# Rewriting the gated mixer of a two-layer decoder trunk: modulation in quarters, v with tokens on partitions, an fp32 spatial product

## The chip, the cores and the metric

The kernel runs on one core of a Trainium2 chip. The metric is the device time of one execution in microseconds; the median of several runs counts. Before the change the median of three runs is 2674.6 us (2672.22, 2674.6 and 2674.74).

## What is computed

A trunk of two layers on one sequence of 1024 tokens, 1024 channels wide, all in float32. Layer 0 mixes tokens with a gated MLP (gMLP), layer 1 with attention; each mixer is followed by a squared-ReLU MLP. Every sub-layer is modulated by shift, scale and gate rows that come from a conditioning vector `c`. The change is in the mixer of layer 0 alone:

```python
def ada_mod(c, w, b):
    m = jax.nn.silu(c) @ w + b                 # w: 1024 x 3072
    shift, scale, gate = jnp.split(m, 3, axis=-1)
    return shift[:, None, :], scale[:, None, :], 1.0 + gate[:, None, :]

def mixer_a(h, w_in, b_in, vn_g, vn_b, w_s, b_s, w_out):    # h = x * (1 + scale) + shift
    uv = jax.nn.gelu(h @ w_in + b_in)          # w_in: 1024 x 2048
    u, v = jnp.split(uv, 2, axis=-1)
    v = layer_norm(v, vn_g, vn_b)              # over the 1024 channels of a token
    v = v.reshape(B, S // CHUNK, CHUNK, A_GROUPS, A_GROUP_DIM)   # 8 chunks of 128 tokens, 16 groups of 64
    w_causal = jnp.where(causal, w_s, 0.0)     # 16 x 128 x 128, lower triangles
    z = jnp.einsum('gts,bnsgc->bntgc', w_causal, v) + b_s.T[:, :, None]
    return (u * z.reshape(B, S, A_WIDTH)) @ w_out

# the sub-layer: x = layer_norm(ALPHA * x + gate * mixer_a(h, ...))
```

## The kernel before, in words

Products of full precision are made of three fp32r matmuls: each operand is split into a high part (a cast, `split`, L100 to L103, the cast on ACT and the difference on DVE by default) and a low part, and hi·hi, hi·lo and lo·hi are summed in PSUM (`passes`, L345). The attention further on also uses plain fp32 matmuls (L1451, L1473, L1518, L1558); L1558 has 64 columns of stationary operand and writes alternately to the lower and the upper 64 partitions of a bank. Transposes are fp32 matmuls against an identity.

The mixer (L506 to L703) goes through these stages:

- **Modulation** (`ada_steps`, L110 to L183, and `mods`, L547). Shift and scale of sub-layer 0 are made in two halves of 512 channels. For each part and half, eight blocks of 128x512 of `ada_w` are loaded by SP and added on DVE, weighted by a column of silu(c) (L125, L128); the sum over partitions is then made on PE with 16 two-column matmuls of the split sum against ones (L162, L163).
- **h transposed.** `build_hT` (L210) transposes `x` on PE, applies scale and shift on ACT while it leaves PSUM (L221) and splits it. This is done for half 0 of the tokens (512 of them), four channel blocks after each half of the modulation, and then for half 1.
- **v.** `v_unit` loads and splits 128 columns of `w_in`; `v_sum` (L522) multiplies with the weights stationary, so v comes out with channels on partitions; `v_end` (L531) applies bias and GELU on ACT, transposes v back on PE (L536), copies it to `vz` on DVE (L537) and takes the statistics (L541). Units 0 to 3 go first for half 0, then half 1; units 4 to 7 follow for both halves.
- **Normalization and spatial product.** `norm_v` (L627) normalizes `vz` in two channel halves with gain and bias rows, mostly on DVE. `spatial(g)` (L639) splits one group of `vz`, multiplies it by the transposed triangle (three fp32r matmuls into `psz`, 512 columns each), and ACT writes it back to `vz` with the bias.
- **u and gating.** `u_unit` (L649) makes 128 channels of u, channels on partitions. `gate_unit` (L660) transposes z on PE (L667) and multiplies by u on DVE (L668).
- **Output product.** `OutRows` (L456) multiplies u·z by `w_out`; its matmuls are named `psd_wout`. After it comes the MLP.

In the background run further modulation steps (`later`, `tick`, L190 to L197): 88 steps, 64 of which load a block of 256 KB into a ring of two buffers and add it on DVE. `tick(6)` stands after each of the v units 4 to 7 and `tick(7)` in each `u_unit`.

The order of instructions on each engine is fixed when the program is built: a list scheduler places them by its own estimates of their times, except those marked with `tc.keep_in_program_order`, which stay in the order in which they are written. On the chip every engine and SP's queue of transfers go through their lists in that order and wait where an operand isn't ready. PSUM holds three banks called `tr` (transposes and small sums) and five called `mm` (products).

## Time and profile before

| | before |
|---|---|
| median of 3 runs | 2674.6 us (2672.22 to 2674.74) |
| profiled execution, its own time | 2670.79 us |
| its span in the profile | 2669.1 us, mean granted clock 0.991 |
| first v product starts | 26.03 us |
| first `psd_wout` matmul starts | 269.68 us |

The page of the profile gives, per engine, busy time and number of instructions. A timeline row reads: start and length in us, engine, line, operation, output tile and inputs, shapes, count; in brackets the idle time of the engine ahead of it and what ended that. A matmul's row lasts longer than the engine is taken by it, because matmuls are pipelined: its price in a dense stretch is the distance between starts. A row of a table by windows gives the stretch and its length, busy time and number of instructions of PE, PEld (weight loads), DVE, ACT and POOL, and at the end the granted clock of PE, the share of the transfer engines and the GB/s moved.

### The profile page before, as it was taken

The page shows a single profiled execution, that of the slowest core. Times are in us where ns is not written, and L with a number is a line of the kernel's source. Part 1 is how long each engine was busy: PE and PEld are TensorE (multiplying, and loading weights), DVE is VectorE, ACT ScalarE, POOL GpSimd, SP SyncE. Part 2 cuts the span into 40 slices and gives each one's busy share as a digit, 9 for nine tenths or more (in the row PEclk, how much of TensorE's full clock was granted, in tenths as well). Part 3 has the DMA queues.
Part 4 walks back from the last instruction along what each step waited for, and adds up shares of the span by engine and source line. Part 5 has one row for each costly group of instructions (what it writes and reads, how often), then busy time and mean ns, then how long its engine had stood idle before and what let it go on. Part 6 is the DMA issues. An engine that isn't in the chain of part 4 may idle for free. (4 is left out here: it accounts for less than half of the span.)

```text
span 2669.1 us, 36556 instructions
## 1 busy us (share of the span) xinstructions
PE 2587.4 (97%) x13114; PEld 2073.9 (78%) x13114; DVE 1933.7 (72%) x3490; ACT 1269.0 (48%) x2456; POOL 208.5 (8%) x225
## 2 busy tenths in 40 slices
PE   6999999999999998999999999999999999999998
PEld 5777878888788887887777777777776888878887
DVE  6786798787788777443676777767658865677887
ACT  3334376555443445322555555556426555543432
POOL 1011100000000000111122221111100000000000
PEclk9999999999999999999999999999999999999999
DMA  8533326666875643543344454444862654494562
GB/s 269 156 114 117 119 104 233 216 213 222 293 249 174 219 145 125 174 158 103 104 136 121 124 156 121 140 138 130 279 213 102 218 194 147 158 332 163 178 204 87
DMA packets 329771, 457.04 MB, mean 171 GB/s; under 512 B 51388, under 2 KB 176740, under 8 KB 329588
## 3 DMA queue, kind: packets, MB, share of 16 engines
q1 hardware_dynamic: 316532, 408.55, 47.7%
q0 software_dynamic: 13056, 46.14, 4.8%
q8 instruction: 103, 1.69, 0.3%
q14 instruction: 80, 0.66, 0.1%
HBM read 346.00 MB, written 108.61 MB: 170 GB/s over the span
## 5 line engine op out<-in xcount | busy, mean ns | idle before, releaser
L1365 PE MATMUL psqk<-right,left 128*128 128x512 f32 x2016 | 524.3, 405 | 3.3 <-DVE left L103 2.2
L1365 PEld LDWEIGHTS psqk<-right,left 128*128 128x128 f32 x2016 | 364.1, 189 | 97.0 <-issue 15.6
L857 PE MATMUL psua<-right,left 128*128 128x512 f32 x1536 | 364.2, 390 | 3.2 <-ACT right L102 1.7
L1015 PE MATMUL psd<-rhi,lhi 128*128 128x512 f32 x896 | 351.7, 392 | 2.1 <-ACT part L888 2.1
L1015 PE MATMUL psd<-rlo,lhi 128*128 128x512 f32 x896 | 351.0, 392 | 0.3 <-DVE rlo L103 0.2
L1015 PE MATMUL psd<-rhi,llo 128*128 128x512 f32 x896 | 350.9, 392 | 0.0
L857 PEld LDWEIGHTS psua<-right,left 128*128 128x128 f32 x1536 | 287.0, 188 | 65.1 <-ACT right L102 2.6
L103 DVE TENSOR_TENSOR left<-ws,left 128x512 fp32r<-128x512 f32 x224 | 163.2, 730 | 145.8 <-ACT left L102 143.9
L1432 ACT ACTIVATE p<-p,stat 128x256 f32<-128x256 f32 (+2 forms) x384 | 161.8, 423 | 154.5 <-DVE stat L1430 153.7
L1209 PE MATMUL psv<-vwhi,right 128*128 128x512 f32 x672 | 210.6, 395 | 7.2 <-ACT right L102 7.2
L1015 PEld LDWEIGHTS psd<-rhi,lhi 128*128 128x128 f32 x896 | 169.4, 189 | 38.1 <-ACT part L888 3.0
L1015 PEld LDWEIGHTS psd<-rlo,lhi 128*128 128x128 f32 x896 | 169.4, 189 | 36.0 <-DVE rlo L103 1.0
L1015 PEld LDWEIGHTS psd<-rhi,llo 128*128 128x128 f32 x896 | 169.6, 189 | 35.4
L857 PE MATMUL psuc<-right,left 128*128 128x512 f32 x768 | 188.2, 391 | 0.5 <-ACT right L102 0.4
L102 ACT CAST left<-ws 128x512 fp32r<-128x512 f32 x224 | 138.5, 619 | 97.8 <-DVE ws L778 78.7
L128 DVE SCALAR_TENSOR_TENSOR adaacc<-adaw,silu_c,adaacc 128x512 f32<-128x512 f32 x168 | 132.5, 798 | 65.5 <-DMA adaw<-in_ada_w_dram 65.0
L857 PEld LDWEIGHTS psuc<-right,left 128*128 128x128 f32 x768 | 143.4, 188 | 30.9 <-DVE right L103 0.9
L1209 PEld LDWEIGHTS psv<-vwhi,right 128*128 128x128 f32 x672 | 126.4, 189 | 35.6 <-ACT right L102 7.6
L103 DVE TENSOR_TENSOR llo<-lraw,lhi 128x1024 fp32r<-128x1024 f32 x112 | 136.3, 1217 | 1.3 <-ACT lhi L102 1.3
L1209 PE MATMUL psv<-vwlo,right 128*128 128x512 f32 x336 | 132.1, 394 | 0.2 <-DVE vwlo L103 0.2
L1430 DVE CUSTOM_DVE_ANT_0 p<-sc,bias 128x256 f32<-128x256 f32 (+2 forms) x384 | 103.3, 324 | 39.9 <-PE sc L1518 39.9
L102 ACT CAST lhi<-lraw 128x1024 fp32r<-128x1024 f32 x112 | 117.3, 1048 | 7.0 <-PE psua L857 4.3
(267 smaller groups left out, 4452.9 us busy)
## 6 DMA issues: line engine op xcount, KB each, us to landing
lraw<-forms SPq DMA_DIRECT2D x112, 512.0 KB, 4.0
adaw<-in_ada_w_dram SPq DMA_DIRECT2D x192, 256.0 KB, 3.0
up<-in_mlp_w_up_dram SPq DMA_DIRECT2D x64, 512.0 KB, 3.7
forms<-s SPq DMA_DIRECT2D x128, 256.0 KB, 2.5
rraw<-in_mlp_w_down_dram SPq DMA_DIRECT2D x64, 512.0 KB, 4.3
forms<-part SPq DMA_DIRECT2D x96, 256.0 KB, 2.4
vraw<-in_b_w_qkv_dram SPq DMA_DIRECT2D x42, 512.0 KB, 3.8
spill<-acc SPq DMA_DIRECT2D x24, 512.0 KB, 2.7
```

What stands on the lines that cost most here:

```text
L102: first = A.copy(hi, src) if hi_engine is A else hi_engine.tensor_copy(hi, src)
L103: return first, lo_engine.tensor_tensor(lo, src, hi, op=ALU.subtract)
L128: ins = V.scalar_tensor_tensor(acc[:], raw[:], silu_c[:, k : k + 1], acc[:], ALU.mult, ALU.add)
L857: T.matmul(acc, w[:, a, k, :], right[p][:, b, k, :], start=p in (1, 2, 5) and k + a + b == 0, stop=k == 3 and a == 1, skip_group_check=True)
L1015: T.matmul(sums[kind, m][:], l[a][:, k, m * P : (m + 1) * P], r[b][:, k, :], start=p in (1, 5, 2, 3) and kp + k + a + b == 0, stop=kp == K ...
L1209: T.matmul(sums[own, m][:], right[p][:, b, 2 * kp + k, m * P : (m + 1) * P], w[a][:, k, :], start=new and k + a + b == 0, stop=kp + k == 2 ...
L1365: ins = T.matmul(sums[kind][:], w[:, a, k, :], right[p][:, b, k, :], start=p in (1, 2, 5) and k + a + b == 0, stop=k == 3 and a == 1, skip ...
L1430: V.tensor_tensor_reduce(out=pr, in0=src, in1=bias, scale=-0.125, scalar=3e38, op0=ALU.add, op1=ALU.min, accum_out=nm)
L1432: A.activation(pr, pr, AF.Exp, bias=nm, scale=-1.0, accum_out=l)
```

## The change

Shift and scale are made in four quarters of 256 channels. A block is now two rows of 128x256. Of the eight k rows of a quarter DVE adds five; the other three go to PE as fp32 matmuls with the raw 128x128 block stationary and one column of silu(c) moving, summed in PSUM with the DVE part against a column of ones: 16 matmuls for a quarter. All of the first stage (loads, sums, transposes, scaling, splits, the first products) is pinned in its written order.

v is made with tokens on partitions: hT is now the stationary operand and the weights move (`v_sums`), so that no transposing back is needed; the bias is added by DVE from PSUM and GELU runs in place. v is normalized without gain and bias; the gain becomes a column factor and the bias a row sum of the triangle (`shifts`) where z is used. The spatial product is one fp32 matmul per group and chunk with v (64 columns) stationary and the triangle moving, which gives z with channels on partitions; the two groups of a unit go to the two halves of the partitions.

The core of the diff (`ada_steps` loses its special case for sub-layer 0, `build_hT` is gone, `ones_f` is a tile of ones):

```diff
+            def v_split(dh, kk, raw, pin=free):
+                w_units[dh, kk] = [wts.tile([P, 2, HALF], F32R, name=f"winv_{dh}_{kk}_{m}", tag=f"w{m}") for m in ("hi", "lo")]
+                for ins in split(*(t[:] for t in w_units[dh, kk]), raw[:]):
+                    pin(ins)
+            def v_sums(half, dh, k, pin=free):
+                w = w_units[dh, k // 2]
+                for i in range(4):
+                    if k == 0:
+                        sums[half, dh, i] = bank("mm", f"psv_{dh}_{4 * half + i}")
+                    for a, b in ((0, 0), (0, 1), (1, 0)):
+                        pin(T.matmul(sums[half, dh, i][:], hT[half][a][:, k, i * P : (i + 1) * P], w[b][:, k % 2, :],
+                                     start=k == 0 and a + b == 0, stop=k == KD - 1 and a == 1))
+            def v_end(half, dh, stats=True):
+                w = slice(dh * HALF, (dh + 1) * HALF)
+                for i in range(4):
+                    z = vz[:, 4 * half + i, w]
+                    V.tensor_tensor(z, sums.pop((half, dh, i))[:], v_bias[:, w], op=ALU.add)
+                    A.activation(z, z, AF.Gelu_apprx_tanh)
+                    V.bn_stats(st_v[:, 4 * half + i, dh, :], z)
...
+                def load(q):
+                    def block(kk, part):
+                        t = raws[q, part, kk] = ada0.tile([P, 2, QUARTER], F32, name=f"adaw_0_{q}_{part}_{kk}", tag="adaw", bufs=16)
+                        c0 = part * D + q * QUARTER
+                        pin(nc.sync.dma_start(t[:], ada_w[0, 0, kk * QUARTER : (kk + 1) * QUARTER, c0 : c0 + QUARTER]
+                                              .rearrange("(k p) n -> p k n", p=P)))
+                    for kk in range(3):
+                        for part in (1, 0):
+                            block(kk, part)
+                    w = slice(q * QUARTER, (q + 1) * QUARTER)
+                    for i in range(4):
+                        pin(nc.sync.dma_start(tiles[i][:, w], x_in[i * P : (i + 1) * P, w]))
+                    w_raw[q] = v_raw(0, q)
+                    for part in (1, 0):
+                        block(3, part)
...
+                def total(q):
+                    pst = bank("tr", f"psa_0_{q}")
+                    for part in range(2):
+                        for n in range(2):
+                            c = slice(2 * part + n, 2 * part + n + 1)
+                            w = slice(n * P, (n + 1) * P)
+                            for k in range(ON_DVE, KD):
+                                pin(T.matmul(pst[:, c], raws[q, part, k // 2][:, k % 2, w], silu_c[:, k : k + 1], start=k == ON_DVE, stop=False))
+                            pin(T.matmul(pst[:, c], accs[q, part][:, w], ones_f[:, 0:1], start=False, stop=True))
...
+                load(0)
+                add(0, range(ON_DVE))
+                load(1)
+                for q in range(4):
+                    total(q)
+                    psts = [turn(0, k, tiles, pin) for k in (2 * q, 2 * q + 1)]
+                    h = scaled(0, 2 * q, psts[0], pin)
+                    high(0, 2 * q, h, pin)
+                    if q:
+                        v_sums(0, 0, 2 * q - 1, pin)
+                    if q < 3:
+                        add(q + 1, range(2))
+                    low(0, 2 * q, h, pin)
+                    v_split(0, q, w_raw[q], pin)
+                    h = scaled(0, 2 * q + 1, psts[1], pin)
+                    high(0, 2 * q + 1, h, pin)
+                    if q < 3:
+                        add(q + 1, range(2, 3))
+                    low(0, 2 * q + 1, h, pin)
+                    v_sums(0, 0, 2 * q, pin)
+                    if q < 2:
+                        load(q + 2)
+                    if q < 3:
+                        add(q + 1, range(3, ON_DVE))
+                v_sums(0, 0, KD - 1, pin)
...
+                v_end(0, 0)
+                for k in range(KD):
+                    h = scaled(1, k, turn(1, k, others))
+                    high(1, k, h)
+                    low(1, k, h)
+                    v_sums(1, 0, k)
+                v_end(1, 0)
...
+                def shifts():
+                    for b in range(2):
+                        pst = bank("tr", f"psrow_{b}")
+                        for n in range(4):
+                            pair(lambda e, rows_: T.matmul(pst[rows_, n * P : (n + 1) * P], ones_f[:, 0:HEAD], wsT[:, 2 * (4 * b + n) + e, :],
+                                                           start=True, stop=True))
...
+                for half in (1, 0):
+                    for k in range(KD):
+                        if half and k % 2 == 0:
+                            v_split(1, k // 2, v_raw(1, k // 2))
+                        v_sums(half, 1, k)
+                        tick(2)
+                    if half:
+                        shifts()
+                    v_end(half, 1)
+                    norm_v(half)
...
                 def gate_unit(u, ut):
                     w = slice(u * P, (u + 1) * P)
+                    banks = []
+                    for half in (1, 0):
+                        p = bank("mm", f"psz_{u}_{half}")
+                        banks.append((half, p))
                         for n in range(4):
-                            T.transpose(pst[:, n * P : (n + 1) * P], vz[:, 4 * half + n, w], ident[:])
-                        V.tensor_tensor(vz[:, tiles, w], pst[:].rearrange("p (n c) -> p n c", c=P),
+                            pair(lambda e, rows_: T.matmul(p[rows_, n * P : (n + 1) * P], vz[:, 4 * half + n, (2 * u + e) * HEAD : (2 * u + e + 1) * HEAD],
+                                                           wsT[:, 2 * u + e, :], start=True, stop=True))
+                    for half, p in banks:
+                        t = work.tile([P, HALF], F32, name=f"zt_{u}_{half}", tag="h")
+                        t3 = t[:].rearrange("p (n c) -> p n c", c=P)
+                        V.scalar_tensor_tensor(t3, p[:].rearrange("p (n c) -> p n c", c=P), cols[:, o_s + u : o_s + u + 1],
+                                               shift[:, u, :].unsqueeze(1).to_broadcast([P, 4, P]), ALU.mult, ALU.add)
+                        V.tensor_tensor(vz[:, 4 * half : 4 * half + 4, w], t3,
                                         ut[:, half * HALF : (half + 1) * HALF].rearrange("p (n c) -> p n c", c=P), op=ALU.mult)
...
                 uts = [u_unit(0)]
                 for u in range(KD):
-                    for g in range(2 * u, 2 * u + (2 if u < 5 else 6)):
-                        if u <= 5:
-                            spatial(g)
-                    if u + 2 < KD:
-                        uts.append(u_unit(u + 2))
+                    if u + 1 < KD:
+                        uts.append(u_unit(u + 1))
                     gate_unit(u, uts[u])
```

`add(q, ks)` is the DVE sum over the k rows given (two parts, 128x256 each); `turn`, `scaled`, `high` and `low` are one channel block's transposes (PE), scaling (ACT), cast (ACT) and difference (DVE); `v_raw` loads 256x512 of `w_in` by SP; `norm_v(half)` normalizes four 128x1024 tiles on ACT. The output product and all that follows are unchanged.

More of the change, by code (lines that the diff above doesn't have):

```diff
@@ L208, in act_pair @@
         return tuple(act.tile([P, KD, HALF], F32R, name=f"{name}_{m}", tag="act") for m in range(2))
-    def build_hT(j, half, tiles, pair, ks=range(KD), pinned=False):
-        hi, lo = pair
-        for k in ks:
-            pst = bank("tr", f"pst_{j}_{half}_{k}")
-            for n, t in enumerate(tiles):
-                ins = T.transpose(pst[:, n * P : (n + 1) * P], t[:, k * P : (k + 1) * P], ident[:])
-                if pinned and n == 0:
-                    tc.keep_in_program_order(ins)
-            h = work.tile([P, HALF], F32, name=f"h_{j}_{half}_{k}", tag="h")
-            mul, add = ada[j]["mul", k // 4], ada[j]["add", k // 4]
-            A.activation(h[:], pst[:], AF.Identity, bias=add[:, k % 4 : k % 4 + 1], scale=mul[:, k % 4 : k % 4 + 1])
-            split(hi[:, k, :], lo[:, k, :], h[:], hi_engine=V if k % 2 else A)
-            yield
     def rstd_of(dst, var, n, name):
@@ L507, in mixer_a @@
         nonlocal ada_p, vec
+        QUARTER = 2 * P
         with ExitStack() as ph:
@@ L531, in v_end @@
-            def v_end(u, half):
-                vt = work.tile([P, HALF], F32, name=f"vt_{u}_{half}", tag="h")
-                A.activation(vt[:], sums[u, half][:], AF.Gelu_apprx_tanh, bias=cols[:, o_i + KD + u : o_i + KD + u + 1])
-                pst = bank("tr", f"psvt_{u}_{half}")
-                for n in range(4):
-                    T.transpose(pst[:, n * P : (n + 1) * P], vt[:, n * P : (n + 1) * P], ident[:])
-                V.tensor_copy(vz[:, 4 * half : 4 * half + 4, u * P : (u + 1) * P],
-                              pst[:].rearrange("p (n c) -> p n c", c=P))
-                if u % 2:
-                    for i in range(4 * half, 4 * half + 4):
-                        V.bn_stats(st_v[:, i, u // 2, :], vz[:, i, (u - 1) * P : (u + 1) * P])
@@ new lines, in v_end, with turn @@
+            def v_end(half, dh, stats=True):
[5 more added lines that the diff above has]
+                    V.bn_stats(st_v[:, 4 * half + i, dh, :], z)
+            def turn(half, k, tiles, pin=free):
+                pst = bank("tr", f"pst_0_{half}_{k}")
+                for n, t in enumerate(tiles):
+                    pin(T.transpose(pst[:, n * P : (n + 1) * P], t[:, k * P : (k + 1) * P], ident[:]))
+                return pst
@@ new lines, in scaled, with high, low @@
+            def scaled(half, k, pst, pin=free):
+                h = work.tile([P, HALF], F32, name=f"h_0_{half}_{k}", tag="h")
+                m = mods[k // 2]
+                pin(A.activation(h[:], pst[:], AF.Identity, bias=m[:, k % 2 : k % 2 + 1], scale=m[:, 2 + k % 2 : 3 + k % 2]))
+                return h
+            def high(half, k, h, pin=free):
+                pin(A.copy(hT[half][0][:, k, :], h[:]))
+            def low(half, k, h, pin=free):
+                pin(V.tensor_tensor(hT[half][1][:, k, :], h[:], hT[half][0][:, k, :], op=ALU.subtract))
@@ new lines, in shifts @@
+                def shifts():
[4 more added lines that the diff above has]
+                                                           start=True, stop=True))
+                        for n in range(4):
+                            u = 4 * b + n
+                            V.scalar_tensor_tensor(shift[:, u, :], pst[:, n * P : (n + 1) * P], cols[:, o_s + KD + u : o_s + KD + u + 1],
+                                                   shift[:, u, :], ALU.mult, ALU.add)
@@ L639, in spatial @@
-                def spatial(g):
-                    w = slice(g * HEAD, (g + 1) * HEAD)
-                    hi = a1.tile([P, NT, HEAD], F32R, name=f"vhi_{g}", tag="vhi", bufs=2)
-                    lo = a1.tile([P, NT, HEAD], F32R, name=f"vlo_{g}", tag="vlo", bufs=2)
-                    split(hi[:], lo[:], vz[:, :, w])
-                    p = bank("mm", f"psz_{g}")
-                    p3 = p[:].rearrange("p (n c) -> p n c", c=HEAD)
-                    passes(p3, [([t[:, g, :] for t in wsT], [hi[:], lo[:]])])
-                    A.activation(vz[:, :, w], p3, AF.Identity, bias=cols[:, o_s + g : o_s + g + 1])
+                    rstd_of(mv[:, 2, tiles], mv[:, 1, tiles], 4, f"r_v{half}")
```

203 lines of the change are left out of this document (84 added, 119 removed).

## The prediction

> **What bounds the kernel now.** The page comes first, for which engine is full; then a table by windows of the mixer's two parts (up to the last product of units 0 to 3 for half 0 of the tokens, and from there to the output product), of a stretch at half clock and of the output product.
>
> ```profile
> span 2669.1 us, 36556 instructions
> PE 2587.4 (97%) x13114; PEld 2073.9 (78%) x13114; DVE 1933.7 (72%) x3490; ACT 1269.0 (48%) x2456; POOL 208.5 (8%) x225
> ```
> ```profile
> 0.00:10.00 10.00, 0.45 (x1) 0.18 (x1) 3.92 (x11) 1.49 (x2) 0.70 (x6) 1.00 0.69 208
> 10.00:20.00 10.00, 0.73 (x3) 0.64 (x4) 8.63 (x13) 1.24 (x2) 0.00 (x0) 1.00 1.07 385
> 61.37:269.68 208.31, 195.03 (x937) 158.54 (x937) 158.00 (x251) 79.70 (x120) 28.63 (x17) 0.98 0.41 124
> 0.00:61.37 61.37, 38.58 (x163) 31.48 (x163) 39.83 (x61) 18.12 (x25) 10.92 (x10) 0.97 0.88 292
> 46.04:49.45 3.41, 3.41 (x18) 3.41 (x19) 0.70 (x3) 1.83 (x3) 0.00 (x0) 0.50 0.22 87
> 269.68:347.25 77.57, 77.57 (x343) 64.14 (x342) 57.59 (x102) 25.72 (x40) 7.78 (x3) 1.00 0.40 129
> ```
>
> PE is 97% busy, so time is saved only by taking work from PE or by filling its idle time. The output product has none of that: 342 matmuls of 512 columns in 77.57 us, **0.227 us** each, at full clock. The mixer ahead of it is different: in the first 61.37 us PE is busy for 38.58, since it waits for the modulation, whose loads keep the transfer engines 88% busy; in the next 208.31 it is busy for 195.03. Whatever moves the start of the output product (269.68 us) moves the end, since PE is dense behind it and nothing there waits for a clock of its own.
>
> **Part 1, the first stage.** Prices from the PE, ACT and DVE timelines: two-column sums, cold and warm; cold products; cold transposes; scaling, casts of 512 and of 1024 elements, the weight's low part, a 512-wide sum.
>
> ```profile
> 22.05 0.35 PE L162 MATMUL psa<-ones_r,adahi 128*128 128x2 f32 x1
> 22.26 0.35 PE L163 MATMUL psa<-ones_r,adalo 128*128 128x2 f32 x1
> 44.99 0.25 PE L162 MATMUL psa<-ones_r,adahi 128*128 128x2 f32 x1
> 45.10 0.25 PE L163 MATMUL psa<-ones_r,adalo 128*128 128x2 f32 x1
> 28.59 0.63 PE L528 MATMUL psv<-hT,winv_lo 128*128 128x512 f32 x1
> 29.02 0.63 PE L528 MATMUL psv<-hT,winv_hi 128*128 128x512 f32 x1
> 46.44 3.39 PE L216 MATMUL pst<-ident,x 128*128 128x128 f32 x16
> ```
> ```profile
> 23.84 1.63 ACT L221 ACTIVATE h<-pst,ada,ada 128x512 f32<-128x512 f32 x2 [0.56 <-PE pst L216]
> 25.37 0.61 ACT L102 CAST hT<-h 128x512 fp32r<-128x512 f32 x1
> 20.73 1.04 ACT L102 CAST winv_hi<-winv_raw 128x1024 fp32r<-128x1024 f32 x1 [1.14 <-DMA winv_raw<-in_a_w_in_dram]
> ```
> ```profile
> 6.74 0.74 DVE L128 SCALAR_TENSOR_TENSOR adaacc<-adaw,silu_c,adaacc 128x512 f32<-128x512 f32 x1
> 100.16 1.21 DVE L103 TENSOR_TENSOR winv_lo<-winv_raw,winv_hi 128x1024 fp32r<-128x1024 f32 x1
> ```
>
> Start to start, a two-column sum costs 0.21 us while the clock is at half and 0.11 at full clock, a product 0.43 against 0.227, a cold transpose 3.39/16 = 0.21.
>
> Data first. `total(0)` needs eight blocks of 256 KB, four slices of x of 128 KB and 512 KB of weights, 3.1 MB. The window rows moved 2.08 MB by 10 us and 385 GB/s after that, so the last block lands at about **13 us**. Later quarters need 3.1 MB per 8.2 us at that rate, and 16 buffers hold two quarters, so loads stay ahead. SP's queue is pinned with them: the loads of quarter 2 wait there for `total(0)` to free its buffers (near 20 us), and behind them stand the bias row, the column rows and x of half 1. These some 8.5 MB take 22 us at 385 GB/s, to 42 us, and the first that is needed, the bias row, is wanted at 63. Half as many elements in a row of the transfer could cost rate; the 512-byte rows of the old weight load lie in windows of the same GB/s, so I take none.
>
> Then PE. A `total` is 16 fp32 matmuls with a 128x128 stationary block each. The trace's only plain fp32 matmuls are in the attention, and there one source matmul leaves two records (below: 16 for 8). I price a total as 32 two-column sums: 32 x 0.21 = 6.7 us cold, 3.5 warm. From below it is 16 (half of that); I stay with 32 because the recorded weight loads double too.
>
> Quarter 0, cold: total ends at 13 + 6.7 = 19.7. Behind it lie, one after the other, the bias add with its handover (0.5), scaling 0.8, cast 0.6, weight cast 1.0 and the weight's low part 1.2 on DVE, behind which two half-width sums hide: 23.8. Twelve products at 0.43: **29**. Quarters 1 to 3, warm: 3.5 + 8 transposes (0.9 in all) + 24 products (5.5), and about 0.6 until the low part of the weights, which is pinned behind the cast of h, is there: 10.5 each, so 31.5. DVE needs per quarter ten half-width sums (0.4 each, from 0.74), two differences of 0.7 and one of 1.2, under 7 us, and stays under PE. The last twelve products: 2.7. Sum **63.2**, against 61.4 now.
>
> The clock can fall again. In the row 46.04:49.45 it is 0.50, after a wait and 32 two-column sums. The Trainium skill ("TensorE: Matmul & The Clock Gate", Part 1) says that about 3.4 us without enough activity halve the clock until a busy window has passed; this row's length of 3.41 us agrees, and the rule speaks against a stage that puts a 3.5 us train of one-column matmuls into each quarter. From the row: one such window costs up to 3.41/2 = 1.7 us. I put in 3 us for a late warm-up and one relapse: first stage **+5 us** (63.2 + 3 - 61.4), between -7 (totals at half price, which is 8.7 less, and no relapse) and +27 (the clock rival).
>
> **Part 2, from there to the output product.** What goes, in the PE timeline: transposes of z (those of v cost the same), spatial products, and four stalls.
>
> ```profile
> 203.61 1.03 PE L667 MATMUL pszt<-ident,vz 128*128 128x128 f32 x8
> 204.40 0.48 PE L350 MATMUL psz<-vhi,wsT 128*128 128x512 f32 x1
> 205.88 0.63 PE L350 MATMUL psu<-hT,winu_hi 128*128 128x512 f32 x2
> ```
> ```profile
> 169.72 0.48 PE L350 MATMUL psz<-vhi,wsT 128*128 128x512 f32 x1
> 175.95 0.79 PE L350 MATMUL psz<-vlo,wsT 128*128 128x512 f32 x1 [5.75 <-DVE vlo L103]
> 178.25 1.05 PE L350 MATMUL psu<-hT,winu_hi 128*128 128x512 f32 x2
> ```
> ```profile
> 247.95 0.50 PE L350 MATMUL psz<-vhi,wsT 128*128 128x512 f32 x1 [0.19 <-ACT vhi L102]
> 255.05 0.39 PE L350 MATMUL psz<-vlo,wsT 128*128 128x512 f32 x1
> 266.69 1.15 PE L667 MATMUL pszt<-ident,vz 128*128 128x128 f32 x9
> 269.15 0.47 PE L154 MATMUL psa<-adahi,ones_r 128*128 128x512 f32 x1 [1.31 <-DVE vz L668]
> ```
>
> Eight transposes take 204.40 - 203.61 = 0.79, 0.10 each; 64 of v and 64 of z go: **-12.8**. Six spatial matmuls take 1.48, 0.247 each; 16 groups of three go: **-11.8**. Stalls that go with them: 169.72 to 178.25 is 8.5 us for six spatial matmuls (7.0 lost while DVE normalizes and splits); 247.95 to 255.05 is 7.1 us for 3.7 us of work (eight spatial, 15 transposes, one of u); 266.69 to 269.15 is 2.5 for 0.9. Together **-12.0**. In their place stands an ACT normalization of eight 1024-wide tiles, done per half, the second behind `u_unit(0)` and `u_unit(1)` (96 products, 22 us); if the scheduler puts the first z product ahead of those, a wait of about 7 us comes back.
>
> What comes: 128 fp32 matmuls for z and 16 for the row sums, each 64 columns of stationary operand by 128 moving. The attention has exactly this shape, as a PE timeline and its forms in that window show:
>
> ```profile
> 1313.53 1.52 PE L1558 MATMUL pv<-pTs,v 128*64 128x256 f32 x16
> 1314.98 0.93 PE L1518 MATMUL sc<-k,q 64*128 64x128 f32 x8
> ```
> ```profile
> L1558 PE MATMUL pv<-pTs,v 128*64 128x256 f32 x8 | 1.3, 392 | 0.0
> L1558 PE MATMUL pv<-pTs,v 128*64 128x128 f32 x8 | 0.8, 273 | 0.0
> ```
>
> Eight source matmuls, four of 256 and four of 128 columns, take 1.45 us until the next line starts: twelve pieces of 128, 0.121 each. 144 x 0.121 = **+17.4**. The skill's "FP8 and Floating Point Precision", TensorE Precision Notes, counts four passes for true fp32: by that rule alone, with this trace's 0.227 for 512 columns, a piece would cost 0.227 and all of them 32.7. The row shows about half of that, as it would if the pairs that alternate between the two partition halves run side by side; the shape is the same, so I take the row.
>
> New waits: the four banks of `v_sums` are given free by DVE's bias add, four times, while five banks exist. With 0.7 us for a 512-wide DVE operation I put 1 us at each of four boundaries. Ticks are also denser, 32 steps beside 44 us of products of v, and DVE waits for their transfers:
>
> ```profile
> DVE adaacc L128 <- DMA adaw<-in_ada_w_dram: 26.1, 20, 2.7
> ```
>
> That is 26.1 us in 20 waits between 97 and 270 us, none on PE's path today. I put 2 us for weights or banks that come late behind such a wait: new waits **+6** (0 to 20). DVE loses its normalization (24 of 512 wide) and the splits of z, which outweighs the second operation that each half unit's gating gains. The weights' low parts that POOL made for units 0 to 3 are in the 1.2 us of part 1. The last unit's gating stays ahead of the output product, but that begins with channel units 0 to 3, so I cost the tail at nothing; uncovered it is four DVE operations of 0.7, 3 us.
>
> Sum of part 2: -12.8 - 11.8 - 12.0 + 17.4 + 6 = **-13.2**. With part 1 (+5): **-8**. The profiled execution took 2670.8 by its own time for a span of 2669.1, and 3.8 us less than the median, 2674.6. A shift of 8 us gives about 2663 for such an execution and **2666** for the median.
>
> **The rivals.**
> *Cheap totals.* A one-column fp32 matmul costs one weight load (half of my price: -3.4 cold, -1.75 in each of three quarters, -8.7) and the new waits are near nothing (-5). For it: the first stage's DVE sums shrink to 5/8, and DVE is busy for 158 of 208 us in part 2. Against: the two records. Result 2674.6 - 8 - 14 = **2653**.
> *DVE sets the pace.* In the 44 us of v's second channel half DVE has 24 sums of 0.75 (18), 4 weight splits (5), 8 bias adds and statistics (11), three reductions and the triangle's copies (9), about 43, and its transfer waits (24 x 1.3 = 31) come on top; where the queue's order puts a bank's release behind them, PE loses up to 15 us more. Result about **2676**, no change.
> *PE stays at half clock through the first stage* (the slower side). Each of quarters 1 to 3 then costs 6.7 + 1.7 + 24 x 0.43 = 18.7 in place of 10.5, the last products 2.5 more: +27 in place of my +3. It outweighs the gain once more than one quarter runs cold. For it: the two-column sums around 22 us did not raise the clock, products still started 0.43 apart at 29 us. Against: each quarter has over 5 us of dense products. By the same page this needs an idle window in every quarter. Result 2674.6 - 8 + 24 = **2691**.
> *No overlap of the fp32 pairs* (the four-pass rule): +15, **2681**; the same shape in the trace speaks against it.
> *The stalls only move*: the scheduler puts z products ahead of the normalization as it did with the spatial ones; +7, **2673**.
>
> **How the numbers follow.** Forecast 0.43; cheap totals 0.22; DVE's pace 0.12; moved stalls 0.08; half clock 0.12; no overlap 0.03. About 0.2% (5.3 us) is what a measurement of this kernel can tell from no change. Of the forecast's case 0.40 lies beyond that; with the cheap totals and 0.02 of the moved stalls that is faster 0.64. Same are 0.03 of the forecast, DVE's pace and the rest of the moved stalls, 0.21; slower are the last two, 0.15. The range goes down to 2649 (cheap totals, no new waits, no relapse: 2666.6 - 8.7 - 6 - 3) and up to 2682, past the missing overlap; it leaves out the half-clock case.
>
> **What would show it.** Right: the output product starts near 262 us; `psa` sums of a quarter take about 3.5 us warm with two records a matmul; z products come at 0.12 us each; no PE wait of over 3 us between 65 and 260 us. Wrong: the first stage ends before 55 or after 75 us; the granted clock shows 0.5 in more than two windows up to 70 us; PE waits for `psv` banks or weights behind DVE's `adaacc`; or the output product moves earlier and the end does not, which would mean that a transfer further on sets the pace.

## The result, and the profile after

Beside four runs of the kernel before (median 2673.48 us, 2672.22 to 2674.74) the changed kernel took **2654.43 us** (four runs, 2648.05 to 2659.27): a ratio of 0.9933, with a 95% interval of 0.9913 to 0.9952. Measured twice more beside the kernel before, it gave 0.9952 (0.9936 to 0.9969) and 0.9941 (0.9928 to 0.9955). By these three ratios it is faster by 13 to 18 us, where 8 were forecast. The profiled execution took 2653.4 us by its own time for a span of 2651.7.

The page of the changed kernel, its span and the first lines on the engines:

```profile
span 2651.7 us, 36843 instructions
PE 2588.0 (98%) x13322; PEld 2080.0 (78%) x13322; DVE 1898.6 (72%) x3462; ACT 1259.1 (47%) x2431; POOL 185.6 (7%) x213
```

PE is busy for as long as before (2587.4): the 17.4 us that the span lost are idle time. Where they lie is read from the table by windows. Its first row is the first stage (up to the last product of v's first 512 channels for half 0 of the tokens), the next the way to the output product, then the output product; three stretches at half clock follow, and the last two rows split the second one at the first product of u:

```profile
0.00:70.24 70.24, 55.87 (x259) 48.91 (x260) 29.00 (x68) 18.41 (x25) 0.70 (x6) 0.88 0.72 233
70.24:256.36 186.12, 183.93 (x1050) 150.93 (x1048) 128.99 (x210) 69.37 (x95) 15.11 (x9) 1.00 0.49 147
256.36:334.09 77.73, 77.73 (x344) 64.25 (x343) 62.85 (x109) 25.61 (x40) 7.36 (x3) 1.00 0.40 129
33.38:36.80 3.42, 3.42 (x13) 3.00 (x12) 2.41 (x7) 2.66 (x4) 0.00 (x0) 0.50 1.09 346
43.62:50.45 6.83, 6.83 (x27) 6.15 (x27) 3.50 (x8) 3.64 (x5) 0.00 (x0) 0.50 0.75 257
57.27:64.10 6.83, 6.83 (x24) 5.96 (x24) 2.08 (x3) 4.70 (x6) 0.00 (x0) 0.50 0.46 154
70.24:147.83 77.59, 75.51 (x373) 61.12 (x372) 50.73 (x88) 30.92 (x42) 3.00 (x4) 1.00 0.46 134
147.83:256.36 108.53, 108.42 (x678) 89.81 (x676) 78.26 (x123) 38.45 (x53) 12.11 (x5) 1.00 0.52 157
```

The same split in the kernel before:

```profile
61.37:146.10 84.73, 81.16 (x399) 64.83 (x400) 64.11 (x111) 27.71 (x40) 3.47 (x4) 1.00 0.50 150
146.10:269.68 123.58, 113.87 (x540) 93.71 (x538) 93.89 (x141) 51.99 (x81) 25.16 (x13) 0.97 0.34 107
```

Set against the rows of before, the first stage became **longer** by 8.9 us (70.24 for 61.37), the rest of v shorter by 7.1 (77.59 for 84.73), and u, z and gating shorter by 15.1 (108.53 for 123.58). The output product starts at 256.36 us, 13.3 earlier. Its own length didn't change.

What is behind it took 2651.7 - 256.4 = 2395.3 us, for 2399.4 before. That difference isn't the change's: in two more profiles of the same changed kernel the output product starts at 252.5 and 252.75 us, and what follows takes 2401.3 and 2398.3. Windows of half clock fall differently there from one execution to the next: in these three profiles they add up to 17.1, 27.3 and 23.9 us, the last 10 us of the span left aside. Over all kernels of this study that stretch took from 2392 to 2412 us. So the start of the output product is the better measure of the mixer; the total carries the scatter of all the rest, which is some 10 us between runs of one kernel.

From PE's waits up to 260 us, changed kernel (total in us, times, longest):

```profile
PE psa L595 <- DVE adaacc L586: 5.3, 1, 5.3
...
PE psa L595 <- DMA adaw<-in_ada_w_dram: 2.5, 1, 2.5
...
PE psws L661 <- DMA ws<-in_a_w_s_dram: 1.2, 1, 1.2
PE pst L534 <- ACT h L540: 0.8, 1, 0.8
```

The first two lie ahead of quarter 0. Behind the first stage only the last two are left, 2.0 us together, where the kernel before waited 7.4 us for `vlo` alone. Of the waits that I priced, for `psv` banks and for weights behind DVE's `adaacc`, there is none.

In PE's timeline, total 0 (the first two rows), total 1, and one unit of z with the product behind it:

```profile
16.31 1.42 PE L595 MATMUL psa<-silu_c,adaw 128*128 128x1 f32 x6
18.01 1.42 PE L595 MATMUL psa<-silu_c,adaw 128*128 128x1 f32 x6
...
30.48 0.81 PE L595 MATMUL psa<-silu_c,adaw 128*128 128x1 f32 x6
31.15 0.36 PE L596 MATMUL psa<-ones_f,adaacc 128*128 128x1 f32 x2
31.38 0.81 PE L595 MATMUL psa<-silu_c,adaw 128*128 128x1 f32 x6
...
212.72 1.97 PE L725 MATMUL psz<-wsT,vz 128*64 128x128 f32 x32
214.62 0.73 PE L328 MATMUL psu<-hT,winu_hi 128*128 128x512 f32 x2
```

A column of a total is four source matmuls, and eight records: (18.01 - 16.31)/8 = 0.21 us each cold (before the clock first rises), (31.38 - 30.48)/8 = 0.11 warm. A unit's 16 z products leave 32 records in 1.90 us, 0.119 us a product.

### The profile page after: what moved, and what is told of

It reads as the page before. It is cut to its first block, busy times and chain, and to the rows that moved or that the text cites. A ratio compares the mean times of both kernels' runs of the same rounds, so it can differ in the third digit from the quotient of the medians.

```text
span 2651.7 us, 36843 instructions
## 1 busy us (share of the span) xinstructions
PE 2588.0 (98%) x13322; PEld 2080.0 (78%) x13322; DVE 1898.6 (72%) x3462; ACT 1259.1 (47%) x2431; POOL 185.6 (7%) x213
## 5 line engine op out<-in xcount | busy, mean ns | idle before, releaser
L128 DVE SCALAR_TENSOR_TENSOR adaacc<-adaw,silu_c,adaacc 128x512 f32<-128x512 f32 x140 | 107.1, 765 | 65.4 <-DMA adaw<-in_ada_w_dram 64.7
```

The lines of the kernel that those rows point to most:

```text
L128: ins = V.scalar_tensor_tensor(acc[:], raw[:], silu_c[:, k : k + 1], acc[:], ALU.mult, ALU.add)
```

## The experiments

The theory, called A: the sums that the change gave to PE are what the first stage loses, by their own time and by the clock, which falls behind each train of one-column matmuls; the gain comes from z and from v without transposing back. The rivals: B, as the first expectation states it; that the order in which the sums stand, and not their number, decides; and that the new z owes its gain to something other than two partition halves side by side. Below, the end of the first stage is the start of its last product (60.9 us in the kernel before, 70.0 in the first profile of the changed one), and the output product is where `psd_wout` starts.

**All sums on DVE.** `ON_DVE` goes from 5 to 8, so PE is left with the four one-column matmuls of the DVE part (eight records) per quarter.

```diff
-                ON_DVE = 5
+                ON_DVE = 8
...
-                            pin(T.matmul(pst[:, c], accs[q, part][:, w], ones_f[:, 0:1], start=False, stop=True))
+                            pin(T.matmul(pst[:, c], accs[q, part][:, w], ones_f[:, 0:1], start=ON_DVE == KD, stop=True))
```

> All eight k rows of a quarter are added on DVE; PE keeps the four sums over partitions. Theory A (the first stage is long because of PE's trains of one-column fp32 sums and the half clock behind them): a total shrinks from 32 records to 8, that is from 3.6 to 0.9 us warm and from 6.8 to 1.7 cold, and the half-clock windows after the first 33 us go; DVE's 16 half-width sums (6.7 us) and its three splits (2.6) then set quarters of about 11 us. First stage ends near 60 us in place of 70.2, time about 2644. Theory B (loads and the chain over DVE and ACT set the stage, PE's sums lie beside them): DVE's chain grows by six sums of 0.42 a quarter, the stage ends near 78, time about 2662.

Measured: 2647.56 us, ratio 0.9924 (0.9898 to 0.9951); the first stage ends at 60.3 us, the output product starts at 246.9. The same kernel once more, beside the changed one:

> The version with all eight blocks of every quarter summed by VectorE, once more and in more rounds. If its first stage is set by the arrival of the weights and VectorE's pace, as its first run showed (60.5 us), the first stage ends at 59 to 62 again, with at most two or three windows of half clock behind the warm-up, and the time is 2644 to 2652. If that run was a lucky fall of the half-clock windows, the first stage ends at 65 or later and the time is that of the changed kernel, some 2655.

Measured: 2647.69 us, ratio 0.9925 (0.991 to 0.9939), first stage 60.5, output product 246.6. Its windows (first stage, way to the output product, two stretches at half clock), and PE's longest wait up to 70 us:

```profile
0.00:60.49 60.49, 38.29 (x163) 30.45 (x164) 38.46 (x92) 18.19 (x25) 0.70 (x6) 0.94 0.82 271
60.49:246.61 186.12, 183.92 (x1048) 150.85 (x1047) 130.09 (x212) 70.72 (x97) 15.23 (x9) 1.00 0.48 147
40.20:43.60 3.40, 3.40 (x10) 2.63 (x9) 2.66 (x6) 3.08 (x5) 0.00 (x0) 0.51 1.06 348
50.50:53.90 3.40, 3.40 (x11) 2.72 (x9) 1.86 (x2) 3.33 (x5) 0.00 (x0) 0.50 0.67 228
```

```profile
PE psa L596 <- DVE adaacc L586: 15.4, 4, 10.5
```

The way to the output product is as long as in the changed kernel (186.12 us in both rows), so the whole gain lies in the first stage. PE now waits 15.4 us for DVE's sums, 10.5 of them ahead of quarter 0, and still ends 9.5 us earlier than in the first profile of the changed kernel. DVE had the time, as its waits for the totals in that stretch show, first in the changed kernel, then here:

```profile
DVE mod L598 <- PE psa L596: 24.9, 4, 9.0
```

```profile
DVE mod L598 <- PE psa L596: 5.6, 4, 2.0
```

The two stretches at half clock that are left don't lie behind a train of raw sums, since this kernel has none. PE waited 2.65 us for DVE shortly before the first and 1.69 us before the second, with eight records of sums and eight transposes in between. So a train isn't the only thing behind which the clock falls.

**Two on DVE**: the same edit the other way, `ON_DVE = 2`, with 28 source matmuls for a total.

```diff
-                ON_DVE = 5
+                ON_DVE = 2
...
```

> Two of the eight k rows on DVE, six on PE: 28 fp32 sums of one column a quarter, 56 records. Theory A: the total of quarter 0 takes 11.9 us cold in place of 6.8, the later ones 6.3 warm in place of 3.6, more where the clock is at half; first stage ends at 84 to 92 us, time about 2670 to 2677. Theory B: DVE's chain gets shorter by 2.5 us a quarter, the stage ends at about 70 to 75, time 2653 to 2659.

Measured: 2679.46 us, ratio 1.0037 (1.0017 to 1.0057), the output product at 274.5. The first stage and its half-clock stretches:

```profile
0.00:89.30 89.30, 76.36 (x355) 69.50 (x356) 19.71 (x44) 18.43 (x25) 0.70 (x6) 0.81 0.56 184
35.10:45.30 10.20, 10.20 (x46) 9.91 (x46) 2.16 (x6) 2.12 (x3) 0.00 (x0) 0.50 0.49 158
52.10:65.80 13.70, 13.70 (x56) 12.76 (x56) 4.09 (x8) 3.64 (x5) 0.00 (x0) 0.50 0.38 137
72.60:82.80 10.20, 10.20 (x42) 9.43 (x42) 2.08 (x3) 4.07 (x6) 0.00 (x0) 0.50 0.24 85
```

With 8, 5 and 2 blocks on DVE the stage takes 60, 66 to 70, and 89 us, and 6.8, 10 to 17, and 34 us of it are at half clock. The sums price the stage, and with the longest trains it runs mostly at half clock, as the slower rival of the prediction had it.

**Sums between products.** The raw one-column sums of the next quarter stand between the products of v, one source matmul behind each product; only the DVE part's four stay in a train.

```diff
-            def v_sums(half, dh, k, pin=free):
+            def v_sums(half, dh, k, pin=free, between=iter(())):
...
+                        next(between, None)
...
-                    v_sums(0, 0, 2 * q, pin)
+                    v_sums(0, 0, 2 * q, pin, raw_sums(q + 1) if q < 3 else iter(()))
```

> The same sums on PE, but the twelve raw ones of the next quarter are put between the twelve v products of this one, one after each, so that no train of one-column sums is left (four of them remain together, 0.9 us). Theory A with the clock as a part of it: no half-clock window between the first warm-up and 70 us; quarters of 10.6 us, first stage ends near 64, time about 2648. Rival (the half clock has another cause, such as the gaps at the quarters' ends): the windows stay, first stage at 70, time 2654.

Measured: 2651.34 us, ratio 0.9935 (0.9914 to 0.9957), the output product at 251.05. The first stage, and rows of PE's timeline in it:

```profile
0.00:66.10 66.10, 53.01 (x261) 46.94 (x262) 28.93 (x68) 18.44 (x25) 0.70 (x6) 1.00 0.74 248
```

```profile
24.72 0.42 PE L598 MATMUL psa<-silu_c,adaw 128*128 128x1 f32 x2
25.00 0.77 PE L520 MATMUL psv<-winv_hi,hT 128*128 128x512 f32 x1
25.57 0.42 PE L598 MATMUL psa<-silu_c,adaw 128*128 128x1 f32 x2
...
36.99 1.05 PE L520 MATMUL psv<-winv_hi,hT 128*128 128x512 f32 x2
37.84 0.55 PE L520 MATMUL psv<-winv_lo,hT 128*128 128x512 f32 x1
...
40.65 0.47 PE L520 MATMUL psv<-winv_hi,hT 128*128 128x512 f32 x1
40.96 0.28 PE L598 MATMUL psa<-silu_c,adaw 128*128 128x1 f32 x2
```

No stretch is granted half clock before 683 us: without trains the relapses are gone, which bears out the second half of A, in one profile. (The sums of quarter 0 still stand in a row, but there the clock is cold anyway. The kernel with six blocks on DVE, further on, has a relapse among sums that stand between products.) The gain is smaller than expected, because the clock came up late. From 24.72 to 25.57 one sum and one product take 0.85 us, from 40.65 to 40.96 a product 0.31. At 36.99 two products still take 0.85 us, 0.425 each, which is the cold price. In the changed kernel the sums of 30.48 already run at the warm price. The row for the first stage says 1.00 all the same: the column of granted clocks shows relapses only, and the cold start has to be read from the distance between starts.

**One half at a time.** In the new z, the four products of the lower 64 partitions are pinned ahead of the four of the upper ones.

```diff
-                        for n in range(4):
-                            pair(lambda e, rows_: T.matmul(p[rows_, n * P : (n + 1) * P], vz[:, 4 * half + n, (2 * u + e) * HEAD : (2 * u + e + 1) * HEAD],
-                                                           wsT[:, 2 * u + e, :], start=True, stop=True))
+                        def lower_then_upper(e, rows_):
+                            for n in range(4):
+                                tc.keep_in_program_order(T.matmul(p[rows_, n * P : (n + 1) * P], vz[:, 4 * half + n, (2 * u + e) * HEAD : (2 * u + e + 1) * HEAD],
+                                                                  wsT[:, 2 * u + e, :], start=True, stop=True))
+                        pair(lower_then_upper)
```

> The z products of a bank in another order: the four that go to the lower 64 partitions, then the four for the upper 64, in place of alternating. Theory (alternating pairs run side by side, that is where 0.12 us a piece comes from): 16 source products take 3.7 us a unit in place of 1.9, +14.6 us in eight units, time about 2669, PE being full there. Rival (a piece costs 0.12 by itself): no change, 2654.

Measured: 2663.59 us, ratio 0.9982 (0.997 to 0.9995), the output product at 266.74. A unit of z in PE's timeline:

```profile
206.12 2.57 PE L726 MATMUL psz<-wsT,vz 128*64 128x128 f32 x32
208.61 0.73 PE L328 MATMUL psu<-hT,winu_hi 128*128 128x512 f32 x2
```

A unit takes 2.49 us in place of 1.90, for the same 32 records. Taking turns between the halves is thus worth 0.6 us a unit, 4.7 us in eight. I had expected 3.7 us a unit, no overlap at all. Why it is less shows when fewer records are taken: the first ones of this unit, up to 206.55, and those of a unit in the changed kernel, up to 213.15 us.

```profile
206.12 0.65 PE L726 MATMUL psz<-wsT,vz 128*64 128x128 f32 x4
212.72 0.66 PE L725 MATMUL psz<-wsT,vz 128*64 128x128 f32 x8
```

In the same 0.65 us one half alone starts four records and two halves start eight. Record by record, one half follows itself every 0.109 us in both kernels, but for a longer first step; where the halves take turns, the second starts 0.007 us after the first. A product is two records, so alone it costs 0.218 us, and two side by side cost the same. Four in a row on one half run alone only in part, because their later records overlap with the first of the other half.

The output product is 10 to 14 us later than in the changed kernel. Against the first profile, which has the same stretches of half clock in its first stage, it is 10.4: 4.7 are the z units, 3.0 a new wait for `adahi` and `adalo` near 172 us, and 6.8 us at half clock follow, which cost up to 3.4. This wait isn't the price of a product. The edit also pins the z products, and whether the pins or the longer units moved that wait wasn't tried.

**The old first stage and v with the new z**: the kernel before, with only the new normalization, row sums, fp32 z and gating put in.

```diff
-                            T.transpose(pst[:, n * P : (n + 1) * P], vz[:, 4 * half + n, w], ident[:])
...
+                            pair(lambda e, rows_: T.matmul(p[rows_, n * P : (n + 1) * P], vz[:, 4 * half + n, (2 * u + e) * HEAD : (2 * u + e + 1) * HEAD],
+                                                           wsT[:, 2 * u + e, :], start=True, stop=True))
...
-                    for g in range(2 * u, 2 * u + (2 if u < 5 else 6)):
-                        if u <= 5:
-                            spatial(g)
```

> The kernel before with one part of the change alone: normalization without gain and bias on ACT, row sums of the triangle, fp32 z products, new gating. The first stage and v (units with channels on partitions, transposed back) stay as before. Theory A (the two parts add up: the new spatial part saves PE 18.2 us of products and transposes and about 12 us of stalls for 17 us of fp32 products): output product starts 12 to 14 us earlier than before, near 256, time about 2658. Rival (the gain of the middle comes from v with tokens on partitions and the loads that now lie elsewhere, and the old order of v leaves its stalls): output product near 265, time about 2668.

Measured: 2666.41 us, ratio 0.9982 (0.9972 to 0.9992). Its three parts:

```profile
0.00:61.40 61.40, 36.19 (x162) 29.61 (x162) 39.43 (x61) 17.70 (x24) 10.57 (x10) 0.97 0.93 284
61.40:146.10 84.70, 81.40 (x399) 64.85 (x399) 60.66 (x106) 26.96 (x38) 3.46 (x4) 1.00 0.51 149
146.10:257.09 110.99, 110.65 (x715) 92.48 (x714) 72.76 (x123) 40.84 (x53) 12.31 (x5) 1.00 0.39 119
```

The first two rows are nearly those of the kernel before, the third is 12.6 us shorter and has 0.3 us of idle time left. The new z alone thus brings the output product to where the whole change had it in its first profile: what v wins by losing its transposes (7.1 us) the new first stage spends there. In the other two profiles the whole change is 4.5 us ahead.

The end didn't follow: ten runs are only 5 us faster than before. In this profile what follows takes 2411.9 us, 12.5 more than before. Half clock explains little of it (eight stretches, 34.1 us in all, for five with 30.7 before). PE is idle there for 54.6 us in place of 45.5, and two thirds of this difference are one wait in the attention (here, then in the kernel before):

```profile
PE pT L1536 <- ACT p L1435: 9.3, 4, 3.9
PE pT L1533 <- ACT p L1432: 3.2, 4, 1.1
```

In the other kernels of this study this wait is 2.7 to 5.4 us. What makes it longer here wasn't tried, so this run shows the new z's gain up to the output product and not at the end.

**The new first stage and v with the old z**, the other half: the changed kernel with the old normalization, spatial products and gating put back.

```diff
-                            A.activation(vz[:, i, :], vz[:, i, :], AF.Identity, bias=mv[:, 3, i : i + 1], scale=mv[:, 2, i : i + 1])
...
+                            V.scalar_tensor_tensor(z, z, mv[:, 0, i : i + 1], vg[:, w], ALU.subtract, ALU.mult)
+                            V.scalar_tensor_tensor(z, z, mv[:, 2, i : i + 1], vb[:, w], ALU.mult, ALU.add)
...
+                            T.transpose(pst[:, n * P : (n + 1) * P], vz[:, 4 * half + n, w], ident[:])
...
+                    for g in range(2 * u, 2 * u + (2 if u < 5 else 6)):
+                        if u <= 5:
+                            spatial(g)
```

> The other part alone: quarters, pinned first stage and v with tokens on partitions from the changed kernel; normalization with gain and bias rows on DVE, split, three fp32r spatial products and the transposes of z from the kernel before. Theory A: the first stage costs 8.9 us more, the missing transposes of v give back 6.4, a few us of waits after half 0 of v go; output product near 269 to 272, time about 2672 to 2675, no gain. Rival (the gain hangs on v's new layout): output product near 260, time about 2662.

Measured: 2687.38 us, ratio 1.0054 (1.004 to 1.0068), far from what I expected. The part from the first product of u on, and PE's waits between 70 and 290 us:

```profile
148.50:284.50 136.00, 120.24 (x518) 97.16 (x516) 99.18 (x144) 51.22 (x80) 25.29 (x13) 0.91 0.39 120
```

```profile
PE psa L159 <- ACT adahi L102: 8.3, 2, 6.3
PE psz L328 <- ACT vhi L102: 3.7, 4, 2.1
PE psz L328 <- DVE vlo L103: 3.3, 2, 3.0
```

With the old normalization and spatial products behind the new v, PE waits for 15 us in other places, and the clock falls three times in this part (mean 0.91). So the halves don't add up: the old z costs 123.6 us in its own kernel and 136.0 here. Which of the moved steps makes `adahi` late wasn't tried. What v's new layout is worth by itself is thus shown by no run, only by the windows of the two kernels.

**Six on DVE, between products, other order of loads.** From the third experiment, with `ON_DVE = 6`, the transposes ahead of each total, and row pair 3 of the blocks loaded first:

```diff
-                ON_DVE = 5
+                ON_DVE = 6
...
-                    for kk in range(3):
+                    for kk in (3, 0, 1):
...
-                        block(3, part)
+                        block(2, part)
...
-                    total(q)
                     psts = [turn(0, k, tiles, pin) for k in (2 * q, 2 * q + 1)]
+                    total(q)
```

> What the runs so far point to: six k rows of a quarter on DVE, the eight raw sums on PE put between the v products of the quarter before, the blocks that PE sums loaded first, the transposes ahead of the totals. Theory A: quarter 0's total ends near 17 us, quarters take 9.7 us by PE and 9.0 by DVE, no half clock after the warm-up, first stage ends near 61, time about 2645. Rival (half clock saved in the first stage comes back elsewhere, or DVE's chain stays at the 10.7 us a quarter that it needs with all rows): first stage at 65, time about 2650.

Measured: 2658.49 us, ratio 0.9953 (0.9939 to 0.9966), the first stage 65.2: a miss. Again the sums between cold products hold the clock down, until about 37 us, and one relapse of 3.4 us follows at 51.0, among warm products with sums between them. The changed kernel, measured once more beside it,

> The changed kernel once more on the same chip, for comparison. Theory: first stage ends at 70, output product starts at 256 to 257, what follows takes 2395 to 2400 us depending on how many half-clock windows fall into it; time about 2654. Rival (the extra 4 us that the part behind the output product's start gained in the first profile belong to the change): that part takes 2395 again, below all profiles of other kernels with an equal number of half-clock windows.

gave 2657.68 us, with a first stage of 66.5.

**Mixed.** The lesson of the two: no raw sums between cold products, and none in a train. DVE sums all eight blocks of quarters 0 and 1, and six of quarters 2 and 3, whose last two stand between warm products. The transposes of quarters 1 to 3 also stand ahead of their totals, so against the kernel with all sums on DVE this is two edits.

```diff
-                ON_DVE = 5
+                ON_DVE = (8, 8, 6, 6)
...
-                    total(q)
+                    if not q:
+                        total(q)
                     psts = [turn(0, k, tiles, pin) for k in (2 * q, 2 * q + 1)]
+                    if q:
+                        total(q)
```

> VectorE sums all eight blocks in the first two quarters and six in the last two, whose two blocks' one-column sums stand between products of the quarter before, when the clock is up. If trains of one-column products bring the clock down and sums between wide products do not, and if sums between cold products are what delayed the warm-up in the two interleaved kernels, then the warm-up is as early as with all sums on VectorE, no half-clock window lies between it and the end of the first stage, and the first stage ends at 57 to 60, some 2 us before that of the version with all sums on VectorE: 2643 to 2650. If instead the sums cost as much wherever they stand, the first stage ends some 4 us behind it (64), and the time is 2650 to 2656.

Measured: **2645.68 us**, ratio 0.9922 (0.9906 to 0.9937), the output product at 243.79. Its first stage:

```profile
0.00:58.34 58.34, 39.84 (x197) 32.24 (x198) 35.39 (x84) 18.20 (x25) 0.70 (x6) 1.00 0.84 281
```

There is no half clock before 678 us, and the first stage is the shortest of all, 2.6 us under that of the kernel before. Beside it ran the changed kernel a third time:

> The changed kernel on the same chip as the two others, for a comparison within one call: first stage 66 to 70 us, output product from 252 to 256, time 2653 to 2659; the version with all sums on VectorE should be some 6 to 10 us below it if its gain in the first stage is real.

Measured: 2651.91 us, ratio 0.9941 (0.9928 to 0.9955); its first stage, and the two stretches at half clock in it:

```profile
0.00:66.72 66.72, 51.76 (x258) 45.45 (x258) 28.69 (x68) 18.18 (x25) 0.70 (x6) 0.92 0.74 246
31.70:38.50 6.80, 6.80 (x26) 6.10 (x26) 3.71 (x9) 3.64 (x5) 0.00 (x0) 0.50 0.96 314
45.40:48.80 3.40, 3.40 (x16) 3.21 (x16) 1.63 (x6) 1.59 (x3) 0.00 (x0) 0.50 0.84 318
```

Measured beside each other, the medians stand in the order of their first stages (2645.7, 2647.7, 2651.9 for 58.3, 60.5, 66.7 us), but the intervals of the three ratios overlap. The profiles separate both versions from the changed kernel, whose first stage took from 66.5 to 70.0 in three. The 2 us between the two versions are less than that scatter, and the mixed one has a single profile: that it is the better of the two isn't shown.

## Why the prediction was right, and where not

**What bounds the kernel** held for the change: what moved the output product moved the end, within the scatter of what follows. The old first stage with the new z is the exception, 12.6 us earlier at the output product and 5 at the end.

**Arrival and quarter 0** held. The last block of total 0 came at 13.3 us (PE's 2.5 us wait for `adaw` ends there; forecast 13), the total ended at 19.7 (19.7), the first product started at 23.3 (23.8) and the twelfth ended at 29.4 (29).

**The price of a total** held: two records a source matmul, 0.21 us cold and 0.11 warm. The rival of cheap totals fell, although its time of 2653 is nearly the one measured: right about the new waits, near nothing, and wrong about the price, 8.7 us of its gain.

**Quarters 1 to 3** were forecast at 10.5 us each, 2.7 for the last products, and 3 for a late warm-up and a relapse, 66.2 at the end. In two of three profiles the last product started at 66.5 and 66.7, in the first one at 70.0. The mechanism was the one that I named and the size too small: not one relapse of 3.4 us but 17.1 us of half clock in the first profile (3.42 + 6.83 + 6.83) and 10.2 in each of the others, so my own sign of being wrong, half clock in more than two windows up to 70 us, did show. Of the nine trains of quarters 1 to 3 in these profiles seven have a relapse in them or right behind them; the two others, both of quarter 3, have none. The Trainium skill ("TensorE: Matmul & The Clock Gate", Part 1) says that the window in which activity is counted runs free, so that the same kernel can show different warm-ups. The trace agrees: PE's first instructions at the warm price start at 30.3, 28.5 and 28.7 us in the three profiles.

One reading was wrong: ahead of the row 46.04:49.45 stand 16 two-column sums and not 32, behind a wait of 2.6 us for `adahi`, so the old trace already had a relapse behind half as many narrow records and a wait.

The versions with fewer sums on PE show that the sums are the cause: 60.5 us with none but DVE's totals, 58.3 with few left, placed between warm products.

**Part 2** came out at -22.2 us where -13.2 was forecast, and this is the step that failed: the sum of new waits. I had put +6 for banks freed four times by DVE and for weights behind denser ticks; the waits measured are 0. Why no bank came late I can only argue: `v_sums` spends three matmuls on a bank before it needs the next, as long as DVE takes to free one. DVE waited 34.1 us for blocks of `ada_w` in this part, for 31.3 before, and PE waited for none of it.

The other terms, by the two windows: for u and z the forecast was -6.4 (transposes of z) - 11.8 - 12.0 + 15.5 (128 products at 0.121) = -14.7, and -15.1 was measured. (The 12.0 I had called stalls: 9.6 were idle time, 9.7 before and 0.1 after; part of the rest is the old kernel's half clock from 172.3 to 179.2 us, which falls on the first of my stretches and which I didn't name.) For v it was -6.4 + 1.9 = -4.5, and -7.1 was measured. Of these 2.6 us, 1.5 are idle time that went with the change (84.73 - 81.16 = 3.6 before, 77.59 - 75.51 = 2.1 after), which I had left out; the last 1.1 I don't assign.

**The price of an fp32 product** with 64 stationary columns, 0.121 us from the attention's rows, held at 0.119. The four-pass rule of the Trainium skill ("FP8 and Floating Point Precision", TensorE Precision Notes) taken alone would have given 0.227 by this trace's rows. The experiment with one half at a time shows that both are right: a product that runs alone costs 0.218 us, near that price, and two on the two halves cost no more than one.

**Stalls that move** didn't in this change: behind the first stage no wait is over 1.2 us. The half-old kernel shows that it was no idle fear: there the waits came back in other places, 15 us of them.

**The rival on the slower side** needed a relapse in every quarter that outlasts the dense products. The first half came true in the first profile, the second didn't: each stretch ended after one or two windows. With 28 source sums a quarter in place of 16 it came closest, with 34 of the 48 us from 35 to 83 at half clock, and the kernel became slower than before (1.0037).

So the forecast had the direction and the mixer's structure right; it was 5 to 10 us short because waits that nothing in the trace showed were priced at 6, and idle time that it did show was left out. In the first profile the first stage, 4 us longer than forecast, hid part of that.

## What to carry to other kernels

A bound in a sum that no row supports should lean to nothing where the waiting engine has several banks or buffers in hand, and every idle stretch of the old trace that the change rewrites belongs in the sum. Here work moved to TensorE as trains of narrow matmuls was paid twice, by its records and in most trains by the clock; so sum on VectorE where it has time, or try narrow matmuls between wide ones once the clock is up. Judge a change in an early stage by when the next dense stage starts; here that told versions 6 us apart, where totals scatter by 10.

## What the hardware showed beside this

- Narrow matmuls between wide ones let a raised clock stand in two kernels of three (the third fell once, for 3.4 us), but in both kernels that had them between cold products the clock rose late: products stayed at the cold 0.43 us until 37 to 38 us, where with a train behind twelve products the warm price was there at 30.5.
- The clock fell behind narrow records with PE busy throughout, and also, with few of them, behind waits of 1.7 and 2.65 us.
- fp32 products with 64 stationary columns on the two partition halves run side by side: a record of either half every 0.109 us, whether the other half works or not.
- Half-clock stretches came in lengths of 3.4, 6.8, 10.2 and 13.7 us, and their places vary between executions of one kernel, in the far part of the kernel too.
- Two parts that each run well in their own kernel were slow together: the old z cost 12.4 us more behind the new v (136.0 against 123.6).
